# Pairs of output tiles in the token mixing: a shared sum that grows in one PSUM bank, against a shared sum kept in SBUF

## The chip, the cores and the metric

The kernel runs on one core of a Trainium2 chip. The metric is the time of one execution on the device, in microseconds (us), as the median of several executions. The engines are named as the profile names them: PE is the matrix engine and PEld its weight load, DVE the vector engine, ACT the scalar engine, POOL the general one, SP the queue that issues most of the DMAs. PSUM is the memory into which PE writes and adds; DVE and ACT read it.

## The reference, cut to what matters

One decoder layer on 512 tokens of width 1024, all in float32:

```python
h = h + 0.5 * rmsnorm(swiglu(rmsnorm(h, ffn1_pre_w)), ffn1_post_w)      # FFN1, inner width 2816
u = rmsnorm(h, mix_pre_w)
y = token_mixing(u, mem, w_in, ...)                                     # the part that changes
h = h + rmsnorm(y @ w_out, mix_post_w)
h = h + 0.5 * rmsnorm(swiglu(rmsnorm(h, ffn2_pre_w)), ffn2_post_w)      # FFN2

def token_mixing(u, mem, w_in, ...):
    proj = u @ w_in                       # 1024 x 10240: columns of all three branches and the gates
    y_hg  = hgrn2(...)                    # a chunked gated recurrence, 4 heads
    y_dil = dilated_attention(...)        # 3 groups x 4 heads, combined by exp(max) weights
    y_mem = memory_attention(...)         # 4 heads on 256 memory tokens
    gates = sigmoid(gate columns + b_gate)
    return sum over the branches of gates[b] * (y_b @ w_branch[b])
```

## The kernel before, in words

**Products.** A float32 product is made of three matmuls on operands that were split into a high and a low part: high by high, low by high, high by low. `split` makes the high part with an ACT instruction (L161) and the low part with a DVE subtraction. `tt` is every DVE operation on two tensors; its line is L158, whatever calls it. A matmul of a pair (below) has 256 columns, a matmul of `mm3` (L341 to L343) 512.

**Pairs.** Where two output tiles of 128 rows come from the same activations, they are computed as a pair by a Strassen-Winograd scheme: seven products of half the depth and half the tokens, not eight. `product` (L361 to L363) is one of the seven: twelve matmuls of 256 columns into one PSUM bank, which can start the bank or add to it. Its weight operand is a quarter of the weights, or a sum of quarters that DVE makes (`wops`); its activation operand is one of seven, made once: quarters of the activations (`xhi`, `xlo` in the rows) and the sums t1 to t4. Products are called 1 to 7; the operands of 4, 5, 6 and 7 are t4, t1, t2 and t3. Every one of the four output quarters is a sum of products, and three of the four share the sum of products 1 and 6.

In `pair`, product 1 goes to bank a and ACT copies it to SBUF (L372). Product 6 goes to bank b, and DVE adds bank and copy to u, the shared sum. Product 5 goes to bank c and is copied (L379), product 7 goes to bank d and is copied (L382). Then product 2 is added into a, 3 into c, 4 into d. `pair_out` makes the four quarters: a copy of a on ACT (L394), and u+c, d-u and v-u on DVE, where v is the difference of the copies of d and c. So a pair takes four banks, four ACT copies of 128x256 and five DVE operations of 128x256. The next product that needs a copied bank is at least two products further on.

Seventy-two pairs run in all: 40 in the two FFNs and 32 in the mixing (6 for the recurrence, 12 for the dilated attention, 2 for the memory queries, 12 for the gates of the branches). `project2` (L401) is the helper by which most of the mixing takes its pairs; the second and third dilated groups call `pair` and `pair_out` themselves (L941), with outputs that are written in a permuted, strided order.

**What sets the order.** The program emits the pairs one after the other, and beside them runs tasks (attention scores, softmax, recurrence, gates) as coroutines that a clock of estimated PE time releases. A scheduler then fixes one order of instructions for every engine; at run time each engine goes through its own list strictly in order, and semaphores make it wait for the others. So an instruction whose operand is late holds up all that stands behind it on its engine. There are five PSUM buffers for products (`ps`) and others for small work (`px`), and 18 weight buffers: a split of weights waits until PE has finished the product nine products earlier, whose buffers it takes.

**Steps of the mixing** in order: the first two heads of the recurrence, preparation of the memory tokens, the other two heads, memory keys and values, the first two heads of dilated attention, memory attention, the other two heads, and then the three branch products with their gates. In the profile this stretch is from about 384 to 990 us.

Of the kernel before, what the change touches and what calls it, by code (L numbers as in the profile page):

```python
# [11 lines left out]
AF = mybir.ActivationFunctionType  # L12
ALU = mybir.AluOpType
# [4 lines left out]
P = 128  # L18
# [34 lines left out]
class Layer:  # L53
# [145 lines left out]
    def prenorm(self, src, gain, t, lat, raw):  # L199
# [33 lines left out]
        self.tt(t3, x12, pts[1], ALU.subtract)  # L233
# [3 lines left out]
        self.tt(t3, x21, t2, ALU.add)  # L237
# [151 lines left out]
    def pair_out(self, r, o1, o2):  # L389


        a, u, c, d, v = r
        nc = self.nc
        for o, f in ((o1[0], lambda o, g: nc.scalar.copy(o, g(a))), (o1[1], lambda o, g: self.tt(o, g(u), g(c), ALU.add)),  # L394
                     (o2[0], lambda o, g: self.tt(o, g(d), g(u), ALU.subtract)), (o2[1], lambda o, g: self.tt(o, g(v), g(u), ALU.subtract))):
            if isinstance(o, tuple):
                f(*o)
            else:
                f(o, lambda x: x)

    def project2(self, ops):  # L401

        r = self.pair(ops)
        y1, y2 = self.slot(), self.slot()
        self.pair_out(r, (y1[:, :HT], y1[:, HT:]), (y2[:, :HT], y2[:, HT:]))
        return y1, y2
# [503 lines left out]
    def mixing(self, a, ready, nbias):  # L910
# [9 lines left out]
        def dil_pair(hp):  # L920
# [87 lines left out]
def layer_kernel(ctx, tc, a, nbias, hmask, out):  # L1008
# [44 lines left out]
    def follow(dest, w):  # L1053
# [3 lines left out]
        def after(h, t):  # L1057
# [4 lines left out]
            return L.prenorm(h[t], gain, t, LAT['norm'], raw)  # L1062
        return after

    def store(h, t):
        for c, n in ((0, 512), (512, 256), (768, 256)) if t == NT - 1 else ((0, 512), (512, 512)):
# [5 lines left out]
                  reload(lambda t, hf: x[t * P:(t + 1) * P, HALVES[hf]]), follow(h1, a["mix_pre_w"][0]), CHUNKS1, PLAN['early1'], PLAN['plain1'])  # L1072
# [45 lines left out]
```

## Time and profile before

| what | value |
|---|---|
| median of 3 runs | 1367.01 us (1365.49 to 1369.76) |
| the profiled execution | 1367.62 us |
| its span | 1365.8 us, mean granted TensorE clock 0.998 |
| PE busy | 1331.6 us, 97% of the span |
| DVE busy | 1050.7 us, 77% |
| ACT busy | 742.2 us, 54% |
| in the mixing, 384 to 990 us (606.00 us) | PE 600.30, DVE 484.67, ACT 339.47 us |

A row of the profile that names an instruction gives its line, its engine, its operation, what it writes and reads by the names in the program, the shape, and how often. Busy time is the sum of the recorded durations; matmuls overlap in the records, so the distance between the starts of two matmuls, their pitch, is the better measure of what one of them costs. In rows of the timeline the first number is the start in us, the second the duration in us, and a bracket at the end gives the idle time of that engine just before, and what released it.

### The profile page before, as it was taken

The page shows a single profiled execution, that of the slowest core. Times are in us where ns is not written, and L with a number is a line of the kernel's source. Part 1 is how long each engine was busy: PE and PEld are TensorE (multiplying, and loading weights), DVE is VectorE, ACT ScalarE, POOL GpSimd, SP SyncE. Part 2 cuts the span into 40 slices and gives each one's busy share as a digit, 9 for nine tenths or more (in the row PEclk, how much of TensorE's full clock was granted, in tenths as well). Part 3 has the DMA queues.
Part 4 walks back from the last instruction along what each step waited for, and adds up shares of the span by engine and source line. Part 5 has one row for each costly group of instructions (what it writes and reads, how often), then busy time and mean ns, then how long its engine had stood idle before and what let it go on. Part 6 is the DMA issues. An engine that isn't in the chain of part 4 may idle for free.

```text
span 1365.8 us, 24324 instructions
## 1 busy us (share of the span) xinstructions
PE 1331.6 (97%) x9197; PEld 1233.0 (90%) x9197; DVE 1050.7 (77%) x1996; ACT 742.2 (54%) x1527; POOL 107.0 (8%) x140
## 2 busy tenths in 40 slices
PE   6999999999999999999999999999999999999997
PEld 6999999999789888899899999999889999999996
DVE  6887776777798975598888988897478877677765
ACT  6665544555467655355554755566366655445541
POOL 1111111110100000000000100000011111111100
PEclk9999999999999999999999999999999999999999
DMA  9676565554435335334224333335465765655513
GB/s 271 141 182 184 148 156 142 143 151 125 168 94 177 96 98 163 123 102 117 63 78 124 100 95 93 108 94 154 135 190 135 186 181 151 152 139 148 146 47 139
DMA packets 238123, 185.76 MB, mean 136 GB/s; under 512 B 9109, under 2 KB 198966, under 8 KB 238006
## 3 DMA queue, kind: packets, MB, share of 16 engines
q1 hardware_dynamic: 224246, 160.02, 39.5%
q0 software_dynamic: 12032, 21.04, 9.4%
q10 hardware_dynamic: 1728, 3.15, 0.6%
q8 instruction: 72, 1.18, 0.3%
q14 instruction: 45, 0.37, 0.1%
HBM read 153.73 MB, written 9.47 MB: 119 GB/s over the span
## 4 chain that ended last, share of the span: by engine, by line
PE 87%; DVE 6%; issue 3%; DMA 2%; ACT 1%; POOL 1%; SPq 0%; POOLq 0%; DVEq 0%; ACTq 0%
PE ps L361 17%; PE ps L363 17%; PE ps L362 17%; PE ps L341 6%; PE ps L342 6%; PE ps L343 6%; PE px L341 5%; PE px L342 5%; PE px L343 5%; PE px L348 4%; DVE s L158 2%; PE px L352 1%; DVE w L158 1%; POOL r L181 1%; DVE s L244 1%
## 5 line engine op out<-in xcount | busy, mean ns | idle before, releaser
L161 ACT ACTIVATE w<-sum 128x512 fp32r<-128x512 f32 x288 | 180.2, 631 | 215.9 <-PE ps L362 180.3
L158 DVE TENSOR_TENSOR w<-sum,w 128x512 fp32r<-128x512 f32 x288 | 196.9, 687 | 76.9 <-ACT w L161 75.9
L361 PE MATMUL ps<-xhi,w 128*128 128x256 f32 x864 | 246.3, 285 | 0.9 <-ACT s L379 0.9
L363 PE MATMUL ps<-xhi,w 128*128 128x256 f32 x864 | 244.8, 283 | 0.0
L362 PE MATMUL ps<-xlo,w 128*128 128x256 f32 x864 | 244.4, 283 | 0.0
L161 ACT ACTIVATE w<-st 128x512 fp32r<-128x512 f32 x260 | 162.9, 630 | 126.7 <-PE ps L362 90.0
L158 DVE TENSOR_TENSOR w<-st,w 128x512 fp32r<-128x512 f32 x260 | 177.2, 688 | 39.3 <-ACT w L161 37.9
L158 DVE TENSOR_TENSOR s<-s,s 128x256 f32<-128x256 f32 (+3 forms) x316 | 176.8, 564 | 16.2 <-ACT s L161 4.6
L361 PEld LDWEIGHTS ps<-xhi,w 128*128 128x128 f32 x864 | 165.6, 192 | 3.8 <-ACT s L379 1.2
L362 PEld LDWEIGHTS ps<-xlo,w 128*128 128x128 f32 x864 | 165.6, 192 | 2.4 <-issue 0.2
L363 PEld LDWEIGHTS ps<-xhi,w 128*128 128x128 f32 x864 | 165.5, 192 | 0.0
L158 DVE TENSOR_TENSOR sum<-sum,st 128x512 f32<-128x512 f32 x176 | 120.4, 687 | 10.9 <-issue 5.0
L158 DVE TENSOR_TENSOR s<-s,ps 128x256 f32<-128x256 f32 (+1 forms) x194 | 92.3, 476 | 29.4 <-PE ps L343 24.0
L341 PE MATMUL px<-s,s 128*128 128x512 f32 x288 | 112.6, 391 | 0.0
L342 PE MATMUL px<-s,s 128*128 128x512 f32 x288 | 112.5, 391 | 0.0
L343 PE MATMUL px<-s,s 128*128 128x512 f32 x288 | 112.0, 389 | 0.0
L361 PE MATMUL ps<-t4hi,w 128*128 128x256 f32 x288 | 81.9, 284 | 0.8 <-ACT s L382 0.8
L361 PE MATMUL ps<-t3hi,w 128*128 128x256 f32 x288 | 82.6, 287 | 0.0
L362 PE MATMUL ps<-t3lo,w 128*128 128x256 f32 x288 | 82.0, 285 | 0.0
L361 PE MATMUL ps<-t1hi,w 128*128 128x256 f32 x288 | 81.7, 284 | 0.0
L363 PE MATMUL ps<-t1hi,w 128*128 128x256 f32 x288 | 81.6, 283 | 0.0
L362 PE MATMUL ps<-t2lo,w 128*128 128x256 f32 x288 | 81.5, 283 | 0.0
(186 smaller groups left out, 3344.2 us busy)
## 6 DMA issues: line engine op xcount, KB each, us to landing
st<-in_ffn_w_gu_dram SPq DMA_DIRECT2D x48, 512.0 KB, 4.9
st<-in_w_in_dram SPq DMA_DIRECT2D x48, 512.0 KB, 3.7
st<-in_ffn_w_down_dram SPq DMA_DIRECT2D x44, 512.0 KB, 3.8
sum<-in_ffn_w_gu_dram SPq DMA_DIRECT2D x80, 256.0 KB, 3.4
sh<-in_ffn_w_gu_dram SPq DMA_DIRECT2D x40, 256.0 KB, 3.8
sum<-sh POOLq DMA_DIRECT2D x40, 256.0 KB, 3.6
sum<-st POOLq DMA_DIRECT2D x40, 256.0 KB, 3.3
sum<-in_w_in_dram SPq DMA_DIRECT2D x32, 256.0 KB, 2.9
```

What stands on the lines that cost most here:

```text
L158: self.pin(self.nc.vector.tensor_tensor(out=out, in0=a, in1=b, op=op))
L161: self.pin(self.nc.scalar.activation(hi, src, AF.Copy))
L181: self.nc.gpsimd.tensor_tensor(out=r, in0=v, in1=self.mhalf[:, :1], op=ALU.pow)
L244: self.nc.vector.scalar_tensor_tensor(out=h[hf][:, cs], in0=y[hf][:, cs], scalar=r, in1=h[hf][:, cs], op0=ALU.mult, op1=ALU.add)
L341: mm(out, lhsT=lhs[0], rhs=rhs[0], start=first, stop=False)
L342: mm(out, lhsT=lhs[0], rhs=rhs[1], start=False, stop=False)
L343: mm(out, lhsT=lhs[1], rhs=rhs[0], start=False, stop=last)
L348: self.nc.tensor.matmul(out, lhsT=lhsT, rhs=rhs, start=start, stop=stop, **k)
L352: self.nc.tensor.transpose(out, in_, self.ident)
L361: mm(out, lhsT=lh, rhs=rh, start=first and k == 0, stop=False, skip_group_check=True)
L362: mm(out, lhsT=lh, rhs=rl, start=False, stop=False, skip_group_check=True)
L363: mm(out, lhsT=ll, rhs=rh, start=False, stop=k == 3, skip_group_check=True)
```

## The change

The mixing's 32 pairs take `chain` and `chain_out` in place of `pair` and `pair_out`; the FFNs keep `pair`. In `chain` the order of the products is 1, 5, 6, 2, 7, 3, 4, and three banks are used. Product 1 starts bank a, and ACT copies it (x, L405). Product 5 starts bank c and is copied (w, L407). Product 6 is added into a, which now holds the shared sum, and ACT copies it (z, L409). Product 2 goes to a bank of its own, y. Product 7 is added into a, and ACT copies it with its sign turned (v, L413). Product 3 is added into c, product 4 into a. `chain_out` makes the quarters x+y, z+c and v-w on DVE and minus a on ACT (L424). A pair then has five ACT instructions of 128x256 and three DVE operations.

PE may add to bank a only when the copy of its former value has ended. So product 6 waits for x, with product 5 between; product 7 waits for z, with product 2 between; product 4 waits for v, with product 3 between.

For the signs to come out, the operands t3 and t4 of the mixing have the opposite sign. t3 takes the same DVE subtraction with its operands exchanged; t4 is made by a `scalar_tensor_tensor` instead of an addition, once for each of two token tiles.

```diff
+    def chain(self, ops):
+        nc = self.nc
+        s1, s2 = self.slot(), self.slot()
+        x, z, v, w = s1[:, :HT], s1[:, HT:], s2[:, :HT], s2[:, HT:]
+        a, c = self.psum((P, HT)), self.psum((P, HT))
+        self.product(a, ops, 1)
+        nc.scalar.copy(x, a)
+        self.product(c, ops, 5)
+        nc.scalar.copy(w, c)
+        self.product(a, ops, 6, False)
+        nc.scalar.copy(z, a)
+        y = self.psum((P, HT))
+        self.product(y, ops, 2)
+        self.product(a, ops, 7, False)
+        nc.scalar.activation(v, a, AF.Copy, scale=-1.0)
+        self.product(c, ops, 3, False)
+        self.product(a, ops, 4, False)
+        return x, y, z, c, a, v, w
+
+    def chain_out(self, r, o1, o2):
+        x, y, z, c, a, v, w = r
+        nc = self.nc
+        for o, f in ((o1[0], lambda o, g: self.tt(o, g(x), g(y), ALU.add)), (o1[1], lambda o, g: self.tt(o, g(z), g(c), ALU.add)),
+                     (o2[0], lambda o, g: nc.scalar.activation(o, g(a), AF.Copy, scale=-1.0)), (o2[1], lambda o, g: self.tt(o, g(v), g(w), ALU.subtract))):
...
     def project2(self, ops):
-        r = self.pair(ops)
+        r = self.chain(ops)
...
-                        self.pair_out(self.pair(next(pairs)), views(q), views(k))
+                        self.chain_out(self.chain(next(pairs)), views(q), views(k))
...
-        self.tt(t3, x12, pts[1], ALU.subtract)
+        if chain:
+            self.tt(t3, pts[1], x12, ALU.subtract)
...
-        self.tt(t3, x21, t2, ALU.add)
+        if chain:
+            nc.vector.scalar_tensor_tensor(out=t3, in0=x21, scalar=-1.0, in1=t2, op0=ALU.mult, op1=ALU.subtract)
```

The change leaves PE's list the same up to the first pair of the mixing and again from the output projection on. Three places in ACT's list matter below. The first is a pair of the gates, as most of the last branches have it. ACT before (rows L161 are splits of weights, L899 is the sigmoid of a gate):

```order
L372 COPY s_10296<-ps_10295 128x256
L161 ACTIVATE w_10506<-sum_10501 128x512
L161 ACTIVATE w_10524<-sum_10502 128x512
L379 COPY s_10296<-ps_10339 128x256
L161 ACTIVATE w_10543<-sum_10293 128x512
L382 COPY s_10297<-ps_10357 128x256
L161 ACTIVATE w_10561<-st_10289 128x512
L394 COPY s_10425<-ps_10295 128x256
```

ACT now, the same place:

```order
L161 ACTIVATE w_10433<-st_10241 128x512
L405 COPY s_10247<-ps_10249 128x256
L161 ACTIVATE w_10452<-sum_10450 128x512
L407 COPY s_10248<-ps_10250 128x256
L161 ACTIVATE w_10473<-sum_10470 128x512
L409 COPY s_10247<-ps_10249 128x256
L161 ACTIVATE w_10491<-st_10241 128x512
L161 ACTIVATE w_10508<-sum_10245 128x512
L413 ACTIVATE s_10248<-ps_10249 128x256
L161 ACTIVATE w_10525<-sum_10469 128x512
```

The three copies from bank ps_10249, and the one of ps_10250 among them, each stand behind a split that waits for the end of the same product, as L379 and L382 did; three of them now read one bank between products that add to it.

The second place is the first pair of the second two recurrence heads, at about 459 us, while the memory tokens are being prepared. ACT before (L161 rows that read px are splits for the memory tokens, L680 is a copy for the recurrence):

```order
L161 ACTIVATE s_5256<-px_5509 128x2x128
L161 ACTIVATE s_5260<-px_5518 128x2x128
L372 COPY s_5550<-ps_5549 128x256
L379 COPY s_5550<-ps_5608 128x256
L161 ACTIVATE w_5727<-st_5543 128x512
L680 COPY s_5605<-px_5600 128x512
L382 COPY s_5551<-ps_5626 128x256
```

ACT now (L709 is the former L680):

```order
L161 ACTIVATE s_5250<-px_5503 128x2x128
L161 ACTIVATE s_5254<-px_5512 128x2x128
L405 COPY s_5543<-ps_5545 128x256
L161 ACTIVATE w_5720<-st_5537 128x512
L709 COPY s_5595<-px_5590 128x512
L407 COPY s_5544<-ps_5546 128x256
L161 ACTIVATE w_5739<-sum_5737 128x512
L161 ACTIVATE w_5760<-sum_5757 128x512
L409 COPY s_5543<-ps_5545 128x256
```

The first copy of the pair stands at the same point, behind the splits for the memory tokens; the copy z of the shared sum (L409) stands six instructions behind it.

The third place is the end of the second combination of the dilated attention, at about 775 us, where the first gates start. ACT before (L899 is the sigmoid of a gate, L777 the exponential of the combination's weights; a row ACT_TABLE_LOAD loads the function table that the next row needs):

```order
L394 COPY s_9523<-ps_9393 128x256
L161 ACTIVATE w_9602<-sum_9597 128x512
L161 ACTIVATE w_9684<-sum_9598 128x512
L899 ACT_TABLE_LOAD
L899 ACTIVATE s_9523<-s_9523,pcols 128x512
L899 ACTIVATE s_9524<-s_9524,pcols 128x512
L777 ACT_TABLE_LOAD
L777 ACTIVATE wt_9652<-wt_9652 128x8
```

ACT now (L928 is the former L899, L806 the former L777):

```order
L413 ACTIVATE s_9354<-ps_9355 128x256
L928 ACT_TABLE_LOAD
L928 ACTIVATE s_9481<-s_9481,pcols 128x512
L424 ACTIVATE s_9482<-ps_9355 128x256
L806 ACT_TABLE_LOAD
L806 ACTIVATE wt_9606<-wt_9606 128x8
L928 ACT_TABLE_LOAD
L928 ACTIVATE s_9482<-s_9482,pcols 128x512
L405 COPY s_9533<-ps_9535 128x256
L806 ACT_TABLE_LOAD
L806 ACTIVATE wt_9622<-wt_9622 128x8
```

The two sigmoids, which stood together behind one load, now have an exponential between them, so the stretch has four loads where it had two, and three of them stand ahead of the copy x of the next pair (L405).

More of the change, by code (lines that the diff above doesn't have):

```diff
@@ L197, in normed, with prenorm @@
             yield pt
-    def prenorm(self, src, gain, t, lat, raw):
+    def prenorm(self, src, gain, t, lat, raw, chain=False):
         nc = self.nc
@@ L232, in prenorm @@
         nc.vector.scalar_tensor_tensor(out=t2, in0=t1, scalar=-1.0, in1=pts[1], op0=ALU.mult, op1=ALU.subtract)
-        self.tt(t3, x12, pts[1], ALU.subtract)
+        if chain:
+            self.tt(t3, pts[1], x12, ALU.subtract)
+        else:
+            self.tt(t3, x12, pts[1], ALU.subtract)
         for n, x in (("t1", t1), ("t2", t2), ("t3", t3)):
@@ L236, in prenorm @@
             yield LAT['comb']
-        self.tt(t3, x21, t2, ALU.add)
+        if chain:
+            nc.vector.scalar_tensor_tensor(out=t3, in0=x21, scalar=-1.0, in1=t2, op0=ALU.mult, op1=ALU.subtract)
+        else:
+            self.tt(t3, x21, t2, ALU.add)
         self.split(self.xc["t4"][0][:, :, ts], self.xc["t4"][1][:, :, ts], t3)
@@ L1051, in reload, with follow @@
         return go
-    def follow(dest, w):
+    def follow(dest, w, chain=False):
         gain, raw = [], {}
@@ L1061, in after @@
                 nc.sync.dma_start(out=dest[t][hf], in_=h[t][hf])
-            return L.prenorm(h[t], gain, t, LAT['norm'], raw)
+            return L.prenorm(h[t], gain, t, LAT['norm'], raw, chain)
         return after
@@ L1071, in layer_kernel @@
     ready = L.ffn(a["ffn1_w_gu"][0], a["ffn1_w_down"][0], a["ffn1_post_w"][0], [first, second],
-                  reload(lambda t, hf: x[t * P:(t + 1) * P, HALVES[hf]]), follow(h1, a["mix_pre_w"][0]), CHUNKS1, PLAN['early1'], PLAN['plain1'])
+                  reload(lambda t, hf: x[t * P:(t + 1) * P, HALVES[hf]]), follow(h1, a["mix_pre_w"][0], True), CHUNKS1, PLAN['early1'], PLAN['plain1'])
     z = L.mixing(a, ready, nbias)
```

6 lines of the change are left out of this document (1 added, 5 removed).

## The prediction

> **What bounds the kernel now.** I read the page first: the busy times, then the chain of waits that ended last.
>
> ```profile
> PE 1331.6 (97%) x9197; PEld 1233.0 (90%) x9197; DVE 1050.7 (77%) x1996; ACT 742.2 (54%) x1527; POOL 107.0 (8%) x140
> PE 87%; DVE 6%; issue 3%; DMA 2%; ACT 1%; POOL 1%; SPq 0%; POOLq 0%; DVEq 0%; ACTq 0%
> ```
>
> PE is busy nearly always, and holds 87% of the chain. The change touches the mixing, so I asked for that stretch alone, for the norm ahead of it and for the end of the kernel (busy us of PE, PEld, DVE, ACT, POOL, then granted clock, DMA share and GB/s), and for PE's waits in the mixing.
>
> ```profile
> 384.00:990.00 606.00, 600.30 (x4183) 552.27 (x4182) 484.67 (x991) 339.47 (x713) 20.80 (x29) 1.00 0.38 112
> 360.00:384.00 24.00, 20.26 (x110) 16.13 (x110) 21.70 (x42) 15.16 (x38) 5.13 (x8) 1.00 0.27 91
> 1350.00:1360.00 10.00, 6.80 (x42) 5.93 (x40) 6.95 (x15) 3.08 (x10) 0.86 (x1) 0.96 0.28 105
> ...
> PE px L348 <- DVE s L158: 2.2, 3, 1.0
> PE px L348 <- ACT s L585: 1.6, 1, 1.6
> PE px L352 <- DVE s L190: 1.0, 1, 1.0
> PE ps L341 <- ACT w L161: 0.7, 1, 0.7
> ```
>
> In the mixing PE is idle for 606.00 - 600.30 = 5.70 us. Its four kinds of wait add up to 5.5 us, and none is for a copy of a pair or for PSUM. The same seven products per pair remain, so a faster DVE or fewer banks can give back at most about 5.7 us, while any new wait of PE is paid in full.
>
> **What the change removes and adds.** The shapes, apart, in the mixing (count, busy us, mean ns, idle before):
>
> ```profile
> L158 DVE TENSOR_TENSOR s<-s,s 128x256 f32<-128x256 f32 x64 | 28.4, 444 | 0.7 <-ACT s L382 0.6
> L158 DVE TENSOR_TENSOR s<-s,ps 128x256 f32<-128x256 f32 x64 | 28.1, 440 | 2.6 <-PE ps L363 2.4
> L158 DVE TENSOR_TENSOR s<-ps,s 128x256 f32<-128x256 f32 x32 | 15.0, 470 | 1.5 <-PE ps L363 0.9
> L379 ACT COPY s<-ps 128x256 f32<-128x256 f32 x32 | 11.5, 360 | 4.2 <-PE ps L363 4.2
> ```
>
> DVE's pair work is 160 operations of 71.5 us; two of five go, so 64 x 0.447 = 28.6 us of 484.67. ACT gains one copy per pair, 32 x 0.36 = 11.5 us on 339.47. I cost both at nothing: neither engine is PE's, and the waits above belong to scores, norms and weight splits, not to these operations. The cover is PE's own stream; if it goes, the rivals below say what is paid. The bank that is freed is worth nothing either, since no wait of PE was for one.
>
> What has a price is the new dependence. PE waits for x, z and v, and I need the age of a copy when PE wants it. A steady pair of gates shows it:
>
> ```profile
> 825.14 0.28 PE L363 MATMUL ps<-t1hi,w 128*128 128x256 f32 x1
> 825.26 0.28 PE L361 MATMUL ps<-t3hi,w 128*128 128x256 f32 x1
> ...
> 825.34 0.63 ACT L161 ACTIVATE w<-sum 128x512 fp32r<-128x512 f32 x1 [0.81 <-PE ps L362]
> ...
> 825.88 0.35 ACT L379 COPY s<-ps 128x256 f32<-128x256 f32 x1
> ```
>
> The last matmul of product 5 starts at 825.14. A split waits for the same product and goes first, and the copy runs from 825.88 to 826.23, 1.09 us after that start. Matmuls start 0.12 us apart. With one product of twelve between, the next one that needs the bank is due 13 x 0.12 = 1.56 us after that start. One place in FFN1 shows what a wait for a copy costs when nothing is between:
>
> ```profile
> 63.21 0.28 PE L363 MATMUL ps<-xhi,w 128*128 128x256 f32 x1
> ...
> 63.95 0.35 ACT L379 COPY s<-ps 128x256 f32<-128x256 f32 x1
> 64.35 0.19 PEld L361 LDWEIGHTS ps<-xhi,w 128*128 128x128 f32 x1 [1.06 <-ACT s L379]
> 64.35 0.39 PE L361 MATMUL ps<-xhi,w 128*128 128x256 f32 x1 [0.86 <-ACT s L379]
> ...
> 64.58 0.28 PE L362 MATMUL ps<-xlo,w 128*128 128x256 f32 x1
> ```
>
> PE goes on 0.05 us after the copy's end, and its second matmul follows 0.23 us later, not 0.12: a wait costs its length and 0.11 more. So a steady copy is ready at 1.14 us, 0.42 before it is wanted. Now the terms, by the order of the changed kernel.
>
> 1. Steady pairs. Exactly twelve matmuls stand between for 24 of the x, 15 of the z and 22 of the v, and one split of the same product ahead of nearly every copy. These 61 waits cost 0. The slots that those copies take on ACT delay splits for products some nine later, 9 x 1.44 us away. Bounds: below 0 there is nothing to gain; above, a second split ahead (0.52 us more) would miss by 0.10 and cost 0.21 each.
>
> 2. The last three pairs of the gates have eight matmuls between for z and for v, the rest of product 2 or 3 being placed elsewhere. Due after 9 x 0.12 = 1.08, ready at 1.14: 0.06 + 0.11 = 0.17, six times, +1.0. Between 0, if no split is ahead, and 6 x 0.7 = 4 with a split more.
>
> 3. The two memory-query pairs have only five and four transposes between product 6 and product 7.
>
> ```profile
> 788.52 0.85 PE L352 MATMUL px<-ident,s 128*128 128x128 f32 x6
> 789.12 0.36 PE L361 MATMUL ps<-xhi,w 128*128 128x256 f32 x1
> ```
>
> Six take 0.60 us, so product 7 is due 0.62 and 0.52 us after the last start. The copy z is ready between 0.60 (825.34 in place of 825.88) and 1.14. That gives 0 to 0.63, and 0.19 to 0.73; I take +0.8 for both, the middle.
>
> 4. The first pair of the second recurrence step, at 459 us.
>
> ```profile
> 459.42 0.37 ACT L372 COPY s<-ps 128x256 f32<-128x256 f32 x1
> 459.67 0.39 ACT L379 COPY s<-ps 128x256 f32<-128x256 f32 x1
> ...
> 457.85 1.06 PE L348 MATMUL px<-s,s 128*128 128x128 f32 x8
> ```
>
> ACT reaches the copy of product 1 at 459.42, long after the product, behind splits for the memory tokens; nobody minds before. Now product 6 waits for it. PE would be there at about 459.25 (the eight rows end their pitch at 458.66, then a matmul and four transposes); the copy ends at 459.79: 0.59 + 0.11. The copy z then has three splits and two copies ahead, ends about 462.35 as product 7 is due: +0.1. Together +0.8, between 0.3 (ACT runs ahead) and 1.5 (the copy L709 is late).
>
> 5. The first combination of the dilated attention. DVE waits for a DMA, then ACT for DVE, then PE for both:
>
> ```profile
> 652.42 0.23 DVE L158 TENSOR_TENSOR mm<-st,ot 128x4 f32<-128x4 f32 x2 [4.76 <-DMA ot<-x]
> ...
> 652.89 0.36 ACT L777 ACTIVATE wt<-wt 128x8 f32<-128x8 f32 x2 [2.46 <-DVE wt L158]
> ...
> 656.23 0.92 PE L348 MATMUL px<-s,s 128*128 128x256 f32 x3 [1.02 <-DVE s L158]
> ...
> 660.42 0.48 PE L348 MATMUL px<-s,s 128*128 128x256 f32 x1 [1.64 <-ACT s L585]
> ```
>
> The copy v of that pair now stands behind these two exponentials and two splits: it ends near 652.89 + 0.26 + 2 x 0.52 + 0.35 = 654.55, and product 4, due near 652.0, waits 2.6 us. But PE was to lose that time anyway, at 656.23 and 660.42, for the same DMA. The end of the stretch stays with the exponentials near 660.4, with two more matmuls done ahead of it: -0.2. Bounds: -1.1, if DVE's two operations fewer bring the chain forward; +1.4, if product 4's lateness delays the scores that feed the exponentials.
>
> 6. The second combination. PE's idle of 0.72 us ahead of row 769.85 goes, as product 2 and twelve matmuls of 512 columns come before product 6; z and v of that pair then stand behind splits with seven and five matmuls between, about 0.5 and 0.25 late with restarts. Net with that restart's 0.11: -0.1. Two table loads more:
>
> ```profile
> 769.85 0.50 PE L341 MATMUL ps<-s,w 128*128 128x512 f32 x1 [0.72 <-ACT w L161]
> 777.92 0.39 PE L342 MATMUL ps<-s,w 128*128 128x512 f32 x1
> 778.15 0.39 PE L343 MATMUL ps<-s,w 128*128 128x512 f32 x1
> ...
> 774.08 1.28 ACT L899 ACT_TABLE_LOAD   x1 [0.61 <-DVE c L158]
> 775.37 1.34 ACT L899 ACTIVATE s<-s,pcols 128x512 f32<-128x512 f32 x2
> 776.72 1.28 ACT L777 ACT_TABLE_LOAD   x1
> 778.01 0.21 ACT L777 ACTIVATE wt<-wt 128x8 f32<-128x8 f32 x1
> ```
>
> Each is 1.28 us, with the next instruction right behind it. From v's end (about 775.1) three loads, two sigmoids, a copy and an exponential take about 6.0 us to the end of copy x, 781.1. PE meanwhile has product 4, twelve matmuls at 0.23, and products 1 and 5, 7.1 us, until 782.2: hidden by 1.1. Bounds of the term: -0.8 to +1.5.
>
> [...]
>
> 7. The norm. `scalar_tensor_tensor` for an addition, twice on DVE. The nearest row is 748 against 683 ns in the same stretch; PE waits for DVE there, so up to 2 x 0.07: +0.1.
>
> Sum: 0 + 1.0 + 0.8 + 0.8 - 0.2 - 0.1 + 0.1 = +2.4. The profiled execution took 1367.62, so 1370.0; it stands 0.61 above the median of the runs, which makes 1369.4 on their scale, 0.18% slower. About 0.3%, 4.1 us, is what a measurement of this kernel tells from no change, so this counts as the same. Own range of this case: 1366 to 1372.
>
> **The rivals.** *The copies come one split too late in the steady pairs.* For it: ACT must now serve four copies in step with PE and starts each only after a split, the margin is 0.42 us, and one split costs 0.52. Against it: in the order of the steady pairs each split waits for the product of the copy behind it, not for a later one. If half of the 61 waits lose 0.21, that adds 6.4 us: 1375.8; all of them, 1382. It decides once copies slip by more than 0.42. Chance 0.33.
>
> *DVE's relief removes the waits.* DVE is busy for 484.67 of 606.00, and 2.2 of 5.5 us of PE's waits are for its `s`; 28.6 us less could bring the scores forward, and the chain at 652 with them. Against it: those waits hang on a DMA landing and on exponentials. If all 5.7 us go and the new waits are hidden: 1361.3. Chance 0.16.
>
> *The change does nothing*, PE's stream being untouched and every new wait covered: 1367. Chance 0.08.
>
> *The table loads take longer.* If each load held ACT twice for its 1.28 us, copy x would be ready 3.8 us later, 2.7 us after PE wants it: 1372.1. Against it: the row behind each load starts at once. Chance 0.01.
>
> *The clock falls.* If many short waits made the granted clock drop as in the row at 1350 (0.96), PE's 600.30 us would grow by 4%, 25 us: 1392. Against it: 3.74 us of idle PE in 24 us, at 360, left the clock at 1.00. Chance 0.02. [...]
>
> **How the numbers follow.** The sum holds 0.40, of which 0.04 lie above 1371.1. Faster by over 0.3%: 0.16. Within: 0.36 of the sum, 0.08, and 0.01 of the late copies at their mildest, 0.45. Slower: 0.04 + 0.32 + 0.01 + 0.02 = 0.39. The range from 1361.5 to 1379 leaves out about a tenth on either side: the late copies at their worst and the clock above, most of the full relief below.
>
> **What would show it.** PE's waits in the mixing of the changed kernel: next to nothing on lines L405, L409 and L413 in steady pairs; one wait of 0.5 to 0.8 on L405 near 459; one of 2 to 3 us on L413 near 652; waits of 0.1 to 0.7 on L409 in the memory-query pairs and of 0.1 in the last three pairs; none near 782. DVE's busy time in the mixing about 456, ACT's about 354 with the loads. I am wrong if L409 and L413 have dozens of waits, or if the waits at 640 to 660 vanish with nothing in their place.

## The result, and the profile after

The changed kernel takes 1378.25 us (median of 4 runs, 1377.93 to 1380.27) against 1367.84 us beside it (4 runs, 1365.49 to 1369.76): 1.0077 of the time before, with a 95% interval of 1.0063 to 1.0091. It is slower by 10.4 us. That lies inside the range of the prediction, 1361.5 to 1379, but the case it held likeliest, no change that can be measured, did not happen, and the slower rival to which it gave the next chance is not what happened either.

The busy times on the page of the changed kernel:

```profile
PE 1337.8 (97%) x9197; PEld 1238.2 (90%) x9197; DVE 1032.6 (75%) x1932; ACT 755.1 (55%) x1561; POOL 107.6 (8%) x140
```

DVE lost 18.1 us of work and ACT gained 12.9, as the change intends. But PE, with the same 9197 matmuls, is busy for 6.2 us longer. The mixing by itself, in the view by windows (PE, PEld, DVE, ACT, POOL, granted clock, DMA share, GB/s), from 384.10 to 999.54, which holds the same work as 384 to 990 did before, and PE's waits in it:

```profile
384.10:999.54 615.44, 605.99 (x4182) 555.93 (x4181) 465.81 (x925) 352.54 (x747) 20.71 (x29) 0.99 0.37 109
```

```profile
PE ps L368 <- ACT s L413: 2.9, 1, 2.9
PE px L355 <- DVE st L763: 2.1, 1, 2.1
PE ps L349 <- DVE s L158: 1.4, 1, 1.4
PE px L359 <- DVE s L190: 1.2, 1, 1.2
PE px L355 <- ACT s L424: 0.9, 1, 0.9
PE px L359 <- DVE s L158: 0.8, 1, 0.8
```

The stretch is 9.44 us longer. PE's idle time in it is 9.45 us, where it was 5.70: 3.75 more, not 9 or 10. Six single waits make it up; only the first is for one of the copies x, z and v, and the fifth is for the output that ACT now makes (L424). The rest of the loss, 5.69 us, does not look like waiting at all: it is in PE's busy time.

**Where the time went, pair by pair.** I took the start of product 1's first matmul in each of the 32 pairs, after minus before; that is the lag, and its step from one pair to the next is what was lost in between. Times are those of the kernel before.

| place | step, us |
|---|---|
| lag when the first pair of the mixing starts | +0.12 |
| first pair of the second recurrence step, 459 to 466 | +1.23 |
| 466 to 596 | +0.12 |
| the third dilated pair, 596 to 608 | +3.56 |
| the two memory-query pairs and the one behind, 641 to 705: 3.53, -1.83, 0.44 | +2.14 |
| second combination, 762 to 780 | +1.09 |
| the next eight pairs of gates | -0.05 |
| last three pairs of gates, 3 x 0.44 | +1.32 |
| sum: the lag at the end of the mixing | +9.53 |

The last matmul of the kernel is 9.6 us later, the span 10.6 us longer; 1.0 us of the span lies behind the last matmul and I have no explanation for it. In all other pairs the step is 0.00 to 0.03.

**The steady pairs** lose nothing. The timeline of one: the last matmul of product 6, the split that waits for it, the copy z, and the first matmul of product 7:

```profile
833.36 0.28 PE L370 MATMUL ps<-t2hi,w 128*128 128x256 f32 x1
833.56 0.63 ACT L161 ACTIVATE w<-sum 128x512 fp32r<-128x512 f32 x1 [0.55 <-PE ps L369]
834.10 0.35 ACT L409 COPY s<-ps 128x256 f32<-128x256 f32 x1
834.92 0.28 PE L368 MATMUL ps<-t3hi,w 128*128 128x256 f32 x1
```

The last matmul starts at 833.36, the copy ends 1.09 us later at 834.45, so that PE could go on at 834.50; and product 7 starts on its pitch at 834.92, 1.56 us later. These are the numbers that the prediction took from the kernel before, with the margin of 0.42 us.

**A part of PE's busy time** shows in the granted clock. The trace records four stretches of 3.41 us at half clock inside the changed kernel, at 381, 607, 661 and 1020; the profile of before has none between its start and its last 10 us. These rows are the first three and the equally long windows ahead of them:

```profile
377.90:381.31 3.41, 1.59 (x7) 0.99 (x6) 3.37 (x7) 2.58 (x7) 0.34 (x2) 1.00 0.62 216
381.31:384.73 3.42, 3.42 (x13) 2.75 (x12) 2.98 (x6) 0.82 (x3) 1.11 (x3) 0.50 0.54 158
603.18:606.59 3.41, 1.33 (x8) 0.92 (x6) 3.37 (x9) 0.09 (x1) 0.00 (x0) 1.00 0.44 134
606.59:610.01 3.42, 3.42 (x18) 3.42 (x17) 2.58 (x8) 0.63 (x1) 0.00 (x0) 0.50 0.48 143
657.79:661.20 3.41, 1.09 (x9) 1.09 (x10) 3.27 (x18) 2.71 (x7) 0.76 (x1) 1.00 0.07 4
661.20:664.62 3.42, 3.42 (x16) 3.15 (x15) 2.81 (x13) 0.39 (x1) 0.00 (x0) 0.50 0.52 153
```

In each pair of rows PE is idle for 1.8 to 2.3 us of the first and then runs through all of the second at a clock of 0.50, where matmuls of 256 columns start 0.21 us apart and not 0.12. So behind a wait of some 2 us time was lost a second time, by an estimate from these rows up to 1.7 us (half of 3.41), and that second time is booked as busy. The experiments below put the stretch at 607 at 1.50 us and the one at 661 at 1.57. The one at 381 cost 1.1 us, but not out of the 9.5: until then this profiled execution was 0.97 us ahead of the one before, and behind it the lag is +0.12. So the half clock holds about 3.1 of the 5.69 us. The rest I did not break down; some of it is waits too short to show as idle, since a recorded matmul of 256 columns lasts 0.28 us and the next starts after 0.12. The last three pairs lose 0.44 us each with PE booked as busy throughout.

**The place at 600**, which no term of the prediction names. SP loads 256 KB of weights (`sh`) that DVE sums, and POOL sends 4 KB of softmax statistics to DRAM (`x<-st`). After:

```profile
595.40 0.20 ACT L788 ACTIVATION_READ_ACCUMULATOR s<-s,nm 128x1 f32 x1
595.89 0.85 POOL L793 DMA_DIRECT2D x<-st  x1 [17.52 <-ACT s L413]
597.14 0.37 SPq L151 DMA_DIRECT2D sh<-in_w_in_dram  x1
603.17 0.69 DVE L158 TENSOR_TENSOR sum<-sum,sh 128x512 f32<-128x512 f32 x1 [2.32 <-DMA sh<-in_w_in_dram]
606.05 0.48 PE L355 MATMUL px<-s,s 128*128 128x256 f32 x1 [2.08 <-DVE st L763]
```

Before:

```profile
595.58 0.37 SPq L151 DMA_DIRECT2D sh<-in_w_in_dram  x1
596.14 0.19 ACT L759 ACTIVATION_READ_ACCUMULATOR s<-s,nm 128x1 f32 x1
596.63 0.85 POOL L764 DMA_DIRECT2D x<-st  x1 [19.61 <-DVE w L158]
599.43 0.69 DVE L158 TENSOR_TENSOR sum<-sum,sh 128x512 f32<-128x512 f32 x1
```

By then the changed kernel is 1.5 us behind, and the load is issued 1.56 us later, with the rest. But the small transfer is issued 0.74 us earlier: before it stood 1.05 us behind the load, now it stands 1.25 us ahead of it. The reason stands in ACT's list. The transfer carries what four exponentials of ACT leave (the ACCUMULATOR rows show the last of them). Before, a copy and two splits stood between these exponentials; now one split does, and the last is done at 595.6 and not at 596.3. The load then arrives late, DVE waits 2.3 us, PE waits for DVE, and the half clock follows. Two windows of 1 us, both 1.42 us behind the load's issue, show that the load does not share its time with others but starts late. Before:

```profile
597.00:598.00 1.00, 1.00 (x10) 1.00 (x10) 0.77 (x2) 0.23 (x1) 0.48 (x1) 1.00 0.96 287
```

After:

```profile
598.56:599.56 1.00, 1.00 (x11) 1.00 (x10) 0.69 (x1) 0.47 (x3) 0.00 (x0) 1.00 0.00 1
```

The DMAs move 287 GB/s in the one and 1 in the other.

**The memory-query pairs and the first combination**, after:

```profile
657.93 0.24 DVE L158 TENSOR_TENSOR mm<-st,ot 128x4 f32<-128x4 f32 x2 [4.90 <-DMA ot<-x]
659.69 0.36 ACT L413 ACTIVATE s<-ps 128x256 f32<-128x256 f32 x1
660.11 0.38 PE L368 MATMUL ps<-t4hi,w 128*128 128x256 f32 x1 [2.87 <-ACT s L413]
663.25 3.43 PE L355 MATMUL px<-s,s 128*128 128x256 f32 x12
664.99 0.69 DVE L610 TENSOR_REDUCE mmx<-px 128x2 f32<-128x512 f32 x1 [0.97 <-PE px L355]
667.19 1.13 PE L355 MATMUL px<-s,s 128*128 128x256 f32 x4
```

The copy v stands behind exponentials that hang on the DMA, and product 4 waits 2.87 us, as foretold (2 to 3 us). The two waits that it was to replace, 1.02 and 1.64, are gone. But then PE goes on at half clock, DVE has to wait 0.97 us for PE's scores, and from the landing of the DMA to the last matmuls of the chain it is 9.26 us (657.93 to 667.19), where it was 8.00 (652.42 to 660.42). Besides, the landing itself lags by 5.51 us, 0.45 more than the start of this pair (5.06), because the transfers are issued later. The 1.26 and the 0.45 are the two steps 3.53 and -1.83; the 0.44 belongs to the pair behind, which is the first dilated pair of the other two heads.

### The profile page after: what moved, and what is told of

Same layout as the page of the kernel before. It is cut to its first block, busy times and chain, and to the rows that moved or that the text cites. A ratio compares the mean times of both kernels' runs of the same rounds, so it can differ in the third digit from the quotient of the medians.

```text
span 1376.4 us, 24313 instructions
## 1 busy us (share of the span) xinstructions
PE 1337.8 (97%) x9197; PEld 1238.2 (90%) x9197; DVE 1032.6 (75%) x1932; ACT 755.1 (55%) x1561; POOL 107.6 (8%) x140
## 4 chain that ended last, share of the span: by engine, by line
PE 85%; DVE 6%; issue 3%; DMA 3%; ACT 2%; POOL 1%; SPq 0%; POOLq 0%; DVEq 0%; ACTq 0%
PE ps L368 17%; PE ps L369 16%; PE ps L370 16%; PE ps L349 5%; PE ps L348 5%; PE ps L350 5%; PE px L349 5%; PE px L348 5%; PE px L350 5%; PE px L355 4%; DVE s L158 2%; PE px L359 1%; DMA s<-in_ffn_pre_w_dram 1%; POOL r L181 1%; DVE w L158 1%
## 5 line engine op out<-in xcount | busy, mean ns | idle before, releaser
L161 ACT ACTIVATE w<-sum 128x512 fp32r<-128x512 f32 x288 | 180.3, 632 | 217.6 <-PE ps L369 180.1
L161 ACT ACTIVATE w<-st 128x512 fp32r<-128x512 f32 x260 | 163.7, 631 | 125.3 <-PE ps L369 90.4
L158 DVE TENSOR_TENSOR s<-s,s 128x512 f32<-128x512 f32 (+3 forms) x250 | 147.1, 595 | 15.7 <-ACT s L161 4.8
L368 PE MATMUL ps<-t4hi,w 128*128 128x256 f32 x288 | 82.4, 286 | 3.6 <-ACT s L413 2.9
L368 PE MATMUL ps<-t3hi,w 128*128 128x256 f32 x288 | 82.8, 287 | 0.0
L368 PE MATMUL ps<-t2hi,w 128*128 128x256 f32 x288 | 82.3, 286 | 0.0
L370 PE MATMUL ps<-t4hi,w 128*128 128x256 f32 x288 | 81.8, 284 | 0.0
L370 PE MATMUL ps<-t3hi,w 128*128 128x256 f32 x288 | 81.8, 284 | 0.0
```

The lines of the kernel that those rows point to most:

```text
L158: self.pin(self.nc.vector.tensor_tensor(out=out, in0=a, in1=b, op=op))
L161: self.pin(self.nc.scalar.activation(hi, src, AF.Copy))
L368: mm(out, lhsT=lh, rhs=rh, start=first and k == 0, stop=False, skip_group_check=True)
L370: mm(out, lhsT=ll, rhs=rh, start=False, stop=k == 3, skip_group_check=True)
```

## The experiments

Pairs that go back to the old form do so with the signs of the changed kernel: the copy of product 7 and one output take them over. The edits are shown shortened to the lines that matter. "Step" below is the one defined above, against the kernel before. Every step comes from the one profiled execution of its kernel, which need not be a typical one: that of the kernel with old memory-query pairs took 1369.61 us, the least of its ten runs, and that of the kernel with idle matmuls 1379.10, the most of its four.

**All 32 pairs in the old form, the norm as changed.**

```diff
-        r = self.chain(ops)
-        self.chain_out(r, views(y1), views(y2))
+        r = self.pair_f(ops)          # pair; the copy of product 7 with scale=-1.0
+        self.pair_f_out(r, views(y1), views(y2))
```

> Only the signs: the norm is the changed one, but all 32 pairs of the mixing go back to four banks and the old order of products, with the copy of product 7 sign-turned and one quarter made by a scalar_tensor_tensor. Theory (the loss comes from where the new copies meet a late ACT or DVE, and from a halved TensorE clock after the long waits): the loss inside the mixing goes, 1367 to 1370 us, and a half-clock stretch near 381 us, if it is there, is the norm's or chance. Rival (the norm's change and its operands cost the time): 1375 us or more.

Measured: 1370.33 us (10 runs), 1.0012 of before, 0.9998 to 1.0026. The exchanged signs and the norm's `scalar_tensor_tensor` cannot be told from nothing; the median lies 0.3 us above the range expected. Its profiled execution has a half-clock stretch right behind the norm too, at 382.1, so the first of the four stretches of the changed kernel isn't the chain's. At 725 PE has a wait of 1.9 us for DVE's `st`, which the kernel before lacks, and the step there is +1.82: as at 600, DVE had waited for a weight load, 1.87 us. But here the small transfer was issued 1.04 us behind the load (716.92 and 715.88), just as in the kernel before (717.26 and 716.22), where DVE does not wait at this place. So a load can also come late with no small transfer ahead of it. What delays it then stays open.

**The two memory-query pairs in the old form.**

```diff
-        qs = self.project2(next(mq))
+        qs = self.project2(next(mq), False)
```

> Only the two memory-query pairs go back to the old form (with turned signs). Theory (the first combination loses time because copy v stands behind exponentials that wait for a transfer): PE's wait of about 2.9 us on copy v near 657 goes, and of the 2.1 us that the changed kernel has lost over the two pairs (steps of +3.5, -1.8 and +0.4) 1.5 or more come back: 1375 to 1377 us, with the step near 600 still there. Rival (the stretch is held by the transfer's landing in any case): the wait moves to the scores, and the steps over these pairs stay at +2 us.

Measured: 1372.32 us (10 runs), 1.0030 of before (1.0019 to 1.0042), so 5.9 us less than the changed kernel and less than the 1375 to 1377 expected. The longest of PE's waits in the mixing:

```profile
PE px L355 <- DVE st L795: 1.9, 1, 1.9
```

The wait for the copy v is gone, and the steps at these pairs sum to -1.41 in place of +2.14. DVE's wait for the late load at 600 is still there, 2.15 us, and PE's wait behind it, 1.9. But in the profiled execution PE's wait fell across two windows of the clock and no half clock followed: the step there is +1.89, not +3.56. Of these 1.67 us, 0.17 come from the wait, which is 2.08 us in the changed kernel; the other 1.50 come matmul by matmul in the half-clock stretch.

The 3.55 us between -1.41 and +2.14 are more than the new wait. The chain behind the landing is 8.08 us, as it was before the change; and the small transfers ahead of it (from the second issue of `x<-st` until DVE has `ot`) take 5.4 us, where they take 7.6 before and 7.5 after. In the three kernels with new dilated pairs and old memory-query pairs this trip takes 5.2 to 5.5 us, in all others between 7.0 and 8.6. What makes it short I did not find.

**No idle time ahead of product 4.** 24 matmuls of 256 columns, whose result nobody reads, fill PE's wait in the first memory-query pair.

```diff
         self.product(c, ops, 3, False)
+        idle, w4, x4 = self.psum((P, HT)), ops(3), self.xop[3]
+        for i in range(24):
+            nc.tensor.matmul(idle, lhsT=w4[0][:, i % 4, :], rhs=x4[0][:, i % 4, :], ...)
         self.product(a, ops, 4, False)
```

> The changed kernel with 24 idle matmuls of 256 columns, 2.9 us, ahead of product 4 of the first memory-query pair, where PE waits 2.9 us for copy v; their result is not used. Theory that the clock is halved because PE stood idle: the half-clock stretch at 661 to 665 us goes, and the time falls by 0.5 to 1.8 us, though PE does 2.9 us more work. Rival (the clock's fall has nothing to do with this wait, or costs nothing): the same time as the changed kernel, or up to 2.9 us more.

Measured: 1376.94 us (4 runs), 1.0055 of before (1.0034 to 1.0077), an interval that overlaps with that of the changed kernel. Product 4 and the first scores behind it:

```profile
660.47 0.39 PE L368 MATMUL ps<-t4hi,w 128*128 128x256 f32 x1 [0.74 <-ACT s L413]
662.72 1.89 PE L355 MATMUL px<-s,s 128*128 128x256 f32 x8
```

Product 4 starts 2.19 us behind the landing, as in the changed kernel (2.18). The half clock at 661 is gone, so idleness brought it on. From product 4 to the first scores it is 2.25 us and not 3.14, and to the start of the eighth matmul of the scores 3.76 and not 5.33: over the same 26 matmuls the half clock had cost 1.57 us. What the whole chain would gain cannot be read here. Behind the eighth matmul the scheduler placed the rows otherwise, PE waits 1.78 and 1.30 us for ACT, and the last scores start 11.85 us behind the landing, not 9.26. The small transfers took 0.7 us longer too, and the steps at these pairs sum to +4.56. An estimate of the chain in the changed order at full clock: 2.18 to product 4, 2.25 to the first scores, and 3.26 from there to the last as in the next kernel (660.40 to 663.66), 7.69 us in place of 9.26, and less than the 8.00 of before.

**The small transfer issued later.** Six small operations on POOL (the same values added and subtracted again) stand ahead of the first `x<-st`; the other engines' lists are those of the changed kernel.

```diff
+        src = self.small.tile([P, 4, 2], F32, tag="xd", ...)     # hd == 0 only
+        nc.gpsimd.tensor_tensor(out=src, in0=st0, in1=st0, op=ALU.add)
+        ...                                                       # five more
-        nc.gpsimd.dma_start(out=x0..., in_=st0)
+        nc.gpsimd.dma_start(out=x0..., in_=src)
```

> The changed kernel with six small POOL operations ahead of the first 4 KB transfer of the dilated statistics (1 to 4 us), so that it is issued after the weight load of about 597 us, as in the kernel before, and not ahead of it; the lists of PE, ACT, DVE and SP are the same. Theory that this small transfer delays the weight load (it starts to move 2.9 us after its issue, 1.4 before): DVE's wait of 2.3 us and PE's of 2.1 near 603 us go, and the half-clock stretch at 607 with them, 3 to 3.6 us off the changed kernel. Rival (the load is late for another reason): these waits stay, and the time with them.

Measured: 1374.27 us (6 runs), 1.0041 of before (1.0020 to 1.0062); 4.0 us less than the changed kernel. The place at 600:

```profile
596.85 0.37 SPq L151 DMA_DIRECT2D sh<-in_w_in_dram  x1
598.39 0.86 POOL L833 DMA_DIRECT2D x<-xd  x1 [0.30 <-POOL xd L832]
600.85 0.69 DVE L158 TENSOR_TENSOR sum<-sum,sh 128x512 f32<-128x512 f32 x1 [0.28 <-DMA sh<-in_w_in_dram]
```

With the transfer 1.54 us behind the load, the load is there in time and the step of 3.56 us is gone. Nothing but POOL was touched.

**The same collision in the kernel before.** A second 4 KB transfer of the same pattern is sent ahead of the load, to a scratch buffer that nobody reads; the pairs are the old ones.

```diff
+            xd = self.small.tile([P, 4, 2], F32, tag="xd", ...)
+            ...                                                   # two small POOL operations fill it
+            nc.gpsimd.dma_start(out=xx.rearrange("(j p) c -> p j c", p=P), in_=xd)
```

> The kernel before, with one more 4 KB transfer of the same pattern from POOL (two small POOL operations, and the transfer to a scratch tensor that nobody reads), issued about 1.5 us ahead of the weight load of 595.6 us; all other lists are the same. Theory (such a transfer ahead of a weight load delays the load by 2 us or so): DVE waits some 2 us for the load near 599, PE 1 to 2 us for DVE near 602, and the step over that pair is +1 to +3.5 us: 1369 to 1371 us. Rival (the late load in the changed kernel had another reason): no wait there, 1368 us.

Measured: 1372.95 us (7 runs) against 1369.01 (10 runs), 1.0030 (1.0019 to 1.0042). The place, and the windows around the wait:

```profile
593.42 0.86 POOL L762 DMA_DIRECT2D xx<-xd  x1 [0.30 <-POOL xd L760]
595.60 0.37 SPq L151 DMA_DIRECT2D sh<-in_w_in_dram  x1
601.99 0.69 DVE L158 TENSOR_TENSOR sum<-sum,sh 128x512 f32<-128x512 f32 x1 [2.57 <-DMA sh<-in_w_in_dram]
```

```profile
602.52:605.93 3.41, 0.86 (x6) 0.80 (x6) 3.31 (x12) 0.00 (x0) 0.56 (x1) 1.00 0.21 62
605.93:609.35 3.42, 3.42 (x18) 3.42 (x17) 2.48 (x7) 0.89 (x2) 0.00 (x0) 0.50 0.57 154
```

DVE waits 2.57 us for the load, PE 2.6 us for DVE, a half-clock stretch follows, and the step is +4.01 us, above the 1 to 3.5 expected. One small transfer, sent ahead of a load, makes the loss in a kernel without a single changed pair. So the cause at 600 is shown from both sides: the order of these two transfers. How the one holds up the other is not shown.

**The twelve dilated pairs in the old form.**

```diff
-                        self.chain_out(self.chain(next(pairs)), views(q), views(k))
+                        self.pair_f_out(self.pair_f(next(pairs)), views(q), views(k))
```

> The 12 pairs of the dilated attention go back to the old form (with turned signs), the other 20 keep the new one. Theory: the step of 3.6 us near 600 us goes with them; the steps at 459 (1.2 us), in the first memory-query pair (near 650), at the second combination and in the last three gate pairs (0.4 each) stay: 1371 to 1376 us. Rival (every pair in the new form costs a little): 12 of 32 of the loss go, about 4 us, spread evenly, none of it at one place.

Measured: 1374.92 us (4 runs), 1.0044 of before (1.0026 to 1.0061). The step at 600 is +0.28, since ACT and DVE run there as before. The steps at 459 (+1.22) and in the last three pairs (0.42 each) stay, as they must. The memory-query pairs keep their wait (2.1 us) and a half-clock stretch at 657; a third stretch stands at 729, behind a wait of 2.0 us for DVE's `st` at the next pair of heads. There, too, DVE waited for a load (2.04 us) with the small transfer 1.04 us behind it, and the step is +3.49.

**The later transfer and the old memory-query pairs together.**

```diff
         the later transfer (above)
+        qs = self.project2(next(mq), False)
```

> The two edits together: the late small transfer, and the memory-query pairs in the old form. Theory (places add up): the sum of the two gains, about 1371 to 1373 us; left are the steps at 459 (1.2), at the second combination (1.0) and in the last three gate pairs (0.4 each). Rival (clearing one stall lets another of the same size appear): no faster than 1374 us.

Measured: 1370.13 us (10 runs), 1.0017 of before (1.0007 to 1.0027): 8.1 of the 10.4 us are gone, a little more than expected. What is left in its steps are 459 (+1.23), 717 (+0.43), the second combination (+0.80) and the last three pairs (0.42 each); against them stand -2.15 at the memory-query pairs and the one behind, where the trip of the small transfers is short, 5.2 us.

**Seven pairs in the old form, 25 in the new.** As the last, and besides the first pair of the second recurrence step, the last dilated pair and the last three pairs of gates.

```diff
+        first pair of the second recurrence step: pair_f
+        last dilated pair: pair_f
+        both memory-query pairs: pair_f
+        last three pairs of gates: pair_f
         the later transfer (above)
```

> As the one before, and four kinds of pair more in the old form: the first of the second recurrence step, the last dilated pair, and the last three gate pairs; 25 of 32 pairs keep the new form. Theory (steady pairs cost nothing, and DVE's relief is worth nothing): within 1 us of the kernel before, 1367 to 1369 us. Rival 1 (each pair in the new form costs a little): 2 us or more above it. Rival 2 (DVE's relief is worth something once the stalls are gone): 2 us or more below it.

Measured: 1368.04 us (10 runs) against 1368.15 (25 runs), 1.0000 (0.9986 to 1.0014). The loss sat in seven pairs and one transfer. The other 25 pairs cost nothing that shows in the time, with an interval of 1.9 us either way; one of them, the pair behind the memory queries, keeps its step of 0.44. What they take from DVE (it is busy 471.02 us of the 606 here, 484.67 before) shows no worth either, so no version of the chain came out ahead of the kernel before.

**The margin measured.** The copies z and v are made twice in the pairs of gates of the recurrence branch and three times in those of the memory branch; the value is the same.

```diff
-        nc.scalar.copy(z, a)
+        for _ in range(more + 1):
+            nc.scalar.copy(z, a)
```

> The changed kernel with copies z and v made twice in the gate pairs of the recurrence's branch (0.26 us more on ACT before each is done) and three times in those of the memory branch (0.52 more). Theory (a steady copy is ready 0.42 us before PE wants it, and a wait costs its length and 0.11): no step in steady pairs of the first branch, and about 0.2 for each of two waits, 0.4 us a pair, in the second. Rival (the margin is smaller, or a wait that ends just in time already stalls PE): steps in the first branch too.

Measured: 1379.22 us (2 runs), 1.0085 of before (1.0055 to 1.0114). One place in the recurrence branch:

```profile
839.83 0.78 ACT L415 ACTIVATE s<-ps 128x256 f32<-128x256 f32 x2
840.66 0.39 PE L368 MATMUL ps<-t4hi,w 128*128 128x256 f32 x1
```

Two copies end at 840.61, PE goes on at 840.66. The last matmul of product 7 started at 839.09, so product 4 was due at 840.65: one more copy, 0.40 to 0.43 us, uses up the margin to 0.01 us. The two waits of such a pair cost 0.19 us together, nearly all of it the restart. So there is a step in the first branch, which the theory did not expect: it had put the second copy at 0.26 us. Three copies cost 0.47 to 0.49 us a pair, less than two more copies would by that count; there the scheduler had moved two more matmuls in ahead of each wait. The margin of 0.42 is confirmed from both sides: no step without the second copy, and the first wait with it.

## Why the prediction was right or wrong

**Steady pairs (term 1): right.** Predicted 0 for 61 waits; the steps are 0.00, and the margin is the one worked out. With it falls the first rival, copies one split late in the steady pairs, which was to end at 1375.8 to 1382: no such wait is in the trace. That the time came out between these two numbers is chance.

**Last three pairs (term 2): mechanism right, size nearly.** +1.0 predicted, 3 x 0.44 = 1.32 measured. The term had waits for z and v. In the first of these pairs z costs 0.17, as worked out (its copy ends at 928.98, PE goes on at 929.04), and v nothing; but product 6 waits for x, whose copy stands behind two splits and ends at 926.43 (PE goes on at 926.48), 0.22 with the restart.

**First pair of the second recurrence step (term 4): size off, wait wrong.** +0.8 predicted for a wait on the copy x (L405). Measured +1.23, and PE waits ahead of that, for the transposes of the memory tokens:

```profile
459.55 0.37 ACT L405 COPY s<-ps 128x256 f32<-128x256 f32 x1
459.92 0.63 PE L359 MATMUL px<-ident,s 128*128 128x128 f32 x4 [0.76 <-DVE s L158]
```

The copy ends at 459.92, when PE is held by DVE's operand anyway; the new order of the products had drawn these transposes forward, ahead of their input.

**Memory queries and first combination (terms 3 and 5): the failing step.** "But PE was to lose that time anyway" was right for the idle time, 2.87 us in place of 2.66. It was wrong in that one wait in one piece isn't two waits apart: the idle time now lay in one window, the half clock followed, and the chain behind the DMA took 1.26 us longer. The upper bound, +1.4 "if product 4's lateness delays the scores", had the lateness of the scores, though not the clock; the value taken, -0.2, did not. Terms 3 and 5 together were +0.6; measured +2.14. Term 3 has one place named wrongly: the pair with four transposes is not a memory-query pair but the dilated pair behind them. That is why its 0.44, well inside the 0.19 to 0.73 foretold, stays when the memory-query pairs go back to the old form.

**Second combination (term 6): wrong by 1.2 us, not by the table loads.** The prediction let PE's idle 0.72 us go and put -0.1. The timeline after:

```profile
779.04 0.50 PE L349 MATMUL ps<-s,w 128*128 128x512 f32 x1 [1.41 <-DVE s L158]
...
786.00 1.28 ACT L806 ACT_TABLE_LOAD   x1
787.30 0.21 ACT L806 ACTIVATE wt<-wt 128x8 f32<-128x8 f32 x1
...
789.64 0.37 ACT L405 COPY s<-ps 128x256 f32<-128x256 f32 x1
...
790.88 0.28 PE L368 MATMUL ps<-t2hi,w 128*128 128x256 f32 x1
```

The matmuls of 512 columns moved forward, and now wait 1.41 us for the low part that DVE makes: the wait did not go, it doubled. The loads are as predicted: copy x ends at 790.01 and product 6 starts on its pitch at 790.88, 0.9 us later (1.1 predicted). A load took 1.28 us and nothing more: 786.00 + 1.28 is 787.28, and the next row starts at 787.30.

**What was in no term: 3.56 us at 600.** The step that failed is "I cost both at nothing: neither engine is PE's". It asked who waits for DVE and ACT and not what they trigger by being earlier. ACT has more to do, but four exponentials in its list are done 0.7 us sooner; the small transfer of POOL, released by them, went ahead of a weight load that it had followed before. The two experiments with that transfer show it from both sides.

**The clock: dismissed wrongly.** The rival "the clock falls" had a chance of 0.02, priced as a mean clock of 0.96 and dismissed with the row at 360, where 3.74 us of idle PE in 24 us left the clock at 1.00. In that row no window of the clock holds more than 1.47 us of idle time. The mean clock did barely move, 0.998 to 0.993, yet half-clock stretches hold about 3.1 of the 9.5 us: 1.50 at 607 and 1.57 at 661. That they follow waits of 2 to 3 us and not dozens of short ones is what the rival missed. Only one of the four stretches, the one at 661, follows a wait for a PSUM bank's copy (2.87 us); those at 381, 607 and 1020 follow waits of 1.82, 2.08 and 1.99 us for operands that DVE makes.

**DVE's relief (rival): no gain in sum.** ACT's 352.54 us in the mixing is near the 354 foretold. DVE's 465.81 is not near 456: for the same work it lost 18.9 us and not 28.6. That term summed the records of single operations, and neighbours overlap in them: an operation of 0.41 us that starts at 658.42 is followed by the next at 658.75. Of the waits that the relief was to remove those at 656 and 660 went, but only to be replaced.

The sum, term by term: predicted +2.4 us, measured +9.5. The difference is 3.56 at 600, 1.5 more at the memory queries and the pair behind, 1.2 more at the second combination, 0.4 at 459, 0.3 at the end and 0.1 elsewhere.

## What to carry to other kernels

Ask of an engine whose list changes what it will release earlier, and which transfer that then passes on the way to the DMA engines. A wait of PE that stayed whole was dearer here than nearly the same wait cut in two: at 600 one of 2.08 us within one window of the clock made a step of 3.56 us, and one of 1.9 us across a border of two windows a step of 1.89. The second payment is booked as PE's busy time, so compare the granted clock and the pitch of matmuls as well as the waits. A table of steps, the lag of one trace behind the other at the start of each unit of work, finds such places where sums of busy time and of waits do not.

## What was not expected of the hardware

**The granted clock changed on a fixed grid of 3.41 us.** Within one execution every change of the granted clock lies on one grid: in the changed kernel the stretches begin at 381.31, 606.59, 661.20 and 1019.60, and the distances 225.28, 54.61 and 358.40 us are 66, 16 and 105 times 3.4133. Where the grid lies differs from execution to execution. I cut the eleven profiled executions of this study into their windows, 4336 in all from the first full clock to the half clock at the end, and took PE's recorded busy time in each. In all 26 windows that a half-clock window follows, 15 inside the kernels and 11 at their ends, PE was idle for at least 1.77 us of 3.41; of the other 4310, seven had 1.71 to 1.78 us idle and none had more. So in these executions the limit lay near 1.77 us, about half of 3.41. Two of the windows, close to it on either side: the kernel with old memory-query pairs (3.41 - 1.67 = 1.74 us idle),

```profile
601.29:604.70 3.41, 1.67 (x11) 1.29 (x10) 2.67 (x5) 0.89 (x2) 0.00 (x0) 1.00 0.69 223
604.70:608.12 3.42, 3.24 (x25) 3.19 (x26) 3.28 (x12) 0.82 (x2) 0.00 (x0) 1.00 0.53 153
```

and the one with old dilated pairs, at the norm (1.77 us):

```profile
377.15:380.56 3.41, 1.64 (x8) 1.04 (x7) 2.97 (x6) 1.68 (x5) 0.86 (x1) 1.00 0.72 226
380.56:383.98 3.42, 3.42 (x9) 2.63 (x9) 2.98 (x6) 1.73 (x5) 1.45 (x3) 0.50 0.49 156
```

The norm's wait of 1.8 us is in every kernel here, the one before too. A half-clock stretch followed where 1.77 us or more of it fell into one window, as in the second pair of rows, and none where a border cut it, as in the profile of before, where the window from 379.64 to 383.05 holds only 1.47 us of idle time.

**A 4 KB transfer ahead of a 256 KB load held the load up by about 2 us.** DVE waited 2.32 us for the load in the changed kernel and 2.57 in the kernel before with the second small transfer. The DMA engines stood nearly still meanwhile (1 GB/s above). Why the one waits for the other, no view shows. It is not the only way for a load to come late: at 717 two of the kernels above lost 1.9 and 2.0 us with the small transfer behind the load. Nor did I find why the trip of the statistics through DRAM takes 5.2 to 5.5 us in some kernels and 7.0 to 8.6 in others.

**A copy that repeats the one ahead took longer than its neighbours.** ACT's second copy from the same bank into the same buffer added 0.40 to 0.43 us, where a copy that follows a split, as at 833.56 and 834.10 above, ends 0.26 us behind it.
